# An attention and recurrence trunk on one core: PSUM banks of the dense units in turns, products from GpSimd to VectorE, key copies one by one

## Chip, cores and metric

One core of one Trainium2 chip. The metric is the time of one execution on the device in microseconds. The kernel before takes 905.94 us, the median of 3 runs (905.71 to 905.98).

## What is computed

Two layers over x (1024 tokens x 1024 features, float32), each with a normalisation before and after and a residual:

```
for layer in range(2):
    h = rmsnorm(x, pre_norm_w[layer])
    y = attention_mixer(h) if layer == 0 else hgrn2_mixer(h)
    x = x + rmsnorm(y, post_norm_w[layer])

attention_mixer:
    q, k, v, z = split(h @ w_in + b_in)            # 1024, 128, 128, 1024 wide
    q, k = partial_rope(q), partial_rope(k)        # 16 query heads, 2 key heads of 64
    o = softmax over the last 128 keys, with a learned sink per head, times v
    return (o * silu(z)) @ w_out + b_out
```

The second layer is a gated linear recurrence with projections of the same kind; the change does not touch it.

## The kernel before, in words

**Dense work.** Every projection is made of units: 8 "products" (steps over the 1024 features) of 3 matmuls each, which accumulate a 128x512 result in one PSUM bank. Each float32 operand is split into a high and a low part (hi, lo), and the three matmuls are hi·hi, hi·lo and lo·hi. A unit is one block of 128 output features and one half (512) of the tokens (`proj_feat`), or 128 tokens and 512 output features (`proj_nat`). `product` (L218 of the profile; in stretches in which TensorE's order is pinned, all its matmuls appear as L88) counts products in `W["pos"]`. Weights come by DMA into `wraw`, and are split into `whi` (L177 on GpSimd, L179 on ScalarE) and `wlo` (L180 on VectorE).

**PSUM.** The 8 banks are four tags of two banks: "mm" for dense units, "s" for scores, "t" for transposes, "o" for outputs. `mm()` hands a dense unit its bank. A bank comes free when its last reader is done; with two banks of a tag a third user waits for the first one's reader.

**Attention.** The stage of layer 0 weaves attention blocks into the dense units. Before its loop of units, the first half's units run (v, q and k of tokens 0 to 511). Then `fill` lists the rest, in order: the second half's key unit and value unit, four query units of head group 0 for the second half, eight query units of group 1, sixteen gate units (z), then four output units. Beside it stands a plan, a list of (product count, function): after each product the entries that have come due are issued. Block number i (of 32: 2 head groups x 8 query blocks x 2 parities) is due at 29 + 7.1 i products with `scores` (8 matmuls into "s", copy and mask L695/L699, minimum L703, exponentials L705, L707, scaling L710 or L712), 13 products later with `turned` (4 transposes into "t", split by L721 on ScalarE and L722 on VectorE, masks L728 to L736 on GpSimd), and 22 products later with `heads_out` (3 or 4 matmuls into "o", read by L754 and L755). In head group 1 the second parity is followed by L757 on GpSimd, the product of gate and output.

**Query units** (`q_unit`) read the bank with L431 (qh, ScalarE) and L433 (ql, VectorE). For the rotary block (ct 0) the chain is: L422 on ScalarE reads the bank, L424 makes the sine product in two pieces on VectorE, L425 the cosine product in place on GpSimd, L426 adds on VectorE, L427 and L429 split. The parts are stored to DRAM (L436) and loaded again block by block (`queries`, L669). **The key unit** (`k_unit`) reads its bank with L557, rotates on VectorE (L558, L562, L563) and copies each key head's 64 rows to both partition halves: KH on ScalarE (L568), KL on VectorE (L569). In the second half these copies wait in the plan, two pairs per entry, at 30 and 36 products after the unit, and each is queued on ScalarE behind the latest exponential. **The value unit** reads its bank with L587 (vf). **Gate units** (`z_unit`) make L641 (ScalarE), L642 (GpSimd), L646 (VectorE) and, for the group whose output is there already, L648 on GpSimd: output times gate. `new_og` closes the pool with the key work's tiles and opens the tile of group 1's outputs in its place.

**What sets the order.** TensorE's order in this stage is the order of the program. The other engines' queues are ordered by the tile scheduler from priorities and its own simulated times, with the bank's readers at high priority, and run in that fixed order on the chip.

Of the kernel before, what the change touches and what calls it, by code (L numbers as in the profile page):

```python
# [12 lines left out]
F32 = mybir.dt.float32  # L13
# [4 lines left out]
AF = mybir.ActivationFunctionType  # L18
ALU = mybir.AluOpType
# [71 lines left out]
def emit(tc, I, out):  # L91
    nc = tc.nc
    v = InOrder(tc, nc.vector)
# [7 lines left out]
    with top:  # L101
# [13 lines left out]
        pos = const.tile([P, 64], I32, name="pos")  # L115
# [14 lines left out]
        whi = [wp.tile([P, 512], F32R, name=f"whi{i}") for i in range(NW)]  # L130
        wlo = [wp.tile([P, 512], F32R, name=f"wlo{i}") for i in range(NW)]
        wraw = [wp.tile([P, 512], F32, name=f"wraw{i}") for i in range(NR)]
        NS = I["w"].shape[0]
        W_K = 10
        W = {"pos": 0, "plan": [], "split": 0, "fetch": 0, "left": {}, "place": {}, "dmas": {}, "split_ins": {}, "free": list(zip(whi, wlo))}


        FIRST = (0, 2, 1, 3)
# [71 lines left out]
            v.scalar_tensor_tensor(lo, ps, scale, hi.bitcast(F32), op0=ALU.mult, op1=ALU.subtract)  # L210

        def mm(shape=(P, 512), tag="mm"):
            return pp.tile(list(shape), F32, tag=tag, name="psmm")

        def product(ps, k, stat, mov):
# [8 lines left out]
        def later(d, f, block=99):  # L224

            W["plan"].append((W["pos"] + d, f, block))
            W["plan"].sort(key=lambda e: e[0])
# [145 lines left out]
        def layer0():  # L373
# [3 lines left out]
            cosT = ka.tile([P, T], F32, tag="big0", name="cosT")  # L377
# [4 lines left out]
            KH = base.tile([P, 2, T], F32R, name="KH")  # L382
            KL = base.tile([P, 2, T], F32R, name="KL")
# [19 lines left out]
            def q_unit(g, ct, half, ps=None, at=None, sc=None):  # L403
                if ps is None:
                    ps = proj_feat(q_first(g, ct), half)
                with hp():
                    b = bias(2 + 4 * g + ct)
                    cs = slice(half * 512, (half + 1) * 512)
                    if sc is None:
                        sc = scaled(ps, half)  # L410
                    ps = sc
                    if at is None:
                        qh = ka.tile([P, 512], F32R, tag="qh", bufs=2, name="qh")
                        ql = None
                    else:
                        qh, ql = [o0v[:, at + i, :].bitcast(F32R) for i in range(2)]
                    hs = slice(8 * g, 8 * g + 8)
                    own = lambda x: ql if ql is not None else x.bitcast(F32R)
                    if ct == 0:
                        qf = qp.tile([P, 512], F32, tag="th", bufs=3, name="qf") if half else ps  # L420
                        tB = qp.tile([P, 512], F32, tag="th", bufs=3, name="qtB")
                        nc.scalar.activation(qf, ps, AF.Identity, bias=b)  # L422
                        for o, i in ((0, 64), (64, 0)):
                            v.tensor_tensor(tB[o:o + 64], qf[i:i + 64], sinT[o:o + 64, cs], op=ALU.mult)  # L424
                        nc.gpsimd.tensor_tensor(qf, qf, cosT[:, cs], op=ALU.mult)  # L425
                        v.tensor_tensor(qf, qf, tB, op=ALU.add)  # L426
                        nc.scalar.activation(qh, qf, AF.Copy)  # L427
                        ql = own(qf)
                        v.tensor_tensor(ql, qf, qh.bitcast(F32), op=ALU.subtract)  # L429
                    else:  # L430
                        nc.scalar.activation(qh, ps, AF.Identity, bias=b)  # L431
                        ql = own(qp.tile([P, 512], F32, tag="th", bufs=3, name="ql") if half else ps)
                        v.scalar_tensor_tensor(ql, ps, b, qh.bitcast(F32), op0=ALU.add, op1=ALU.subtract)  # L433
                    for l, q in enumerate((qh, ql)):
                        for k, (r, n) in enumerate((((0, 8), (32, 8)), ((8, 16),), ((24, 8), (40, 8)), ((48, 16),))[ct]):
                            nc.sync.dma_start(qdh[hs, 64 * l + r:64 * l + r + n, cs], q[64 * k:64 * k + 8 * n].bitcast(F32))  # L436
# [3 lines left out]
            with pool("start", "right") as sp:  # L440
# [109 lines left out]
                def k_unit(half):  # L550
                    cs = slice(half * 512, (half + 1) * 512)
                    ps = proj_feat(W_K, half)
                    with hp():
                        ps = scaled(ps, half)
                        kr = qp.tile([P, 512], F32, tag="th", bufs=3, name="kr") if half else ps

                        nc.scalar.activation(kr, ps, AF.Identity, bias=hbias[:, 0:1], scale=-0.125)  # L557
                    v.tensor_tensor(kf, kr, cosK[:, cs], op=ALU.mult)  # L558
                    for o in range(4):
                        s1, s2 = slice(32 * o, 32 * o + 8), slice(32 * (o ^ 1), 32 * (o ^ 1) + 8)  # L560
                        s3 = slice(64 * (o % 2), 64 * (o % 2) + 8)
                        v.tensor_tensor(tK[s1], kr[s2], sinT[s3, cs], op=ALU.mult)  # L562
                    v.tensor_tensor(kf, kf, tK, op=ALU.add)  # L563

                    def halves(kv):
                        kr = kf[64 * kv:64 * kv + 64]
                        for o in (0, 64):
                            nc.scalar.activation(KH[o:o + 64, kv, cs], kr, AF.Copy)  # L568
                            v.tensor_tensor(KL[o:o + 64, kv, cs], kr, KH[o:o + 64, kv, cs].bitcast(F32), op=ALU.subtract)  # L569

                    for kv in range(2):
                        if half:
                            def behind(kv):

                                with tc.issue_after(W["exp"].ins):
                                    halves(kv)
                            later(30 + 6 * kv, lambda kv=kv: behind(kv))
                        else:
                            halves(kv)

                def v_unit(half, ps=None, sc=None):
                    if ps is None:
# [52 lines left out]
            with pool("att", "right") as ap:  # L635
                def z_unit(p, half):
                    ps = proj_feat(20 + 2 * (p ^ 4), half)
                    with hp():
                        ps = scaled(ps, half)
                        th = ka.tile([P, 512], F32, tag="qh", bufs=2, name="th")  # L640
                        nc.scalar.activation(th, ps, AF.Tanh, bias=hbias[:, 10 + p:11 + p], scale=0.5)  # L641
                        nc.gpsimd.tensor_scalar(th, th, 0.5, 0.5, op0=ALU.mult, op1=ALU.add)  # L642
                        o = og[p // 4][:, p % 4, half * 512:(half + 1) * 512]

                        early = p >= 4
                        v.scalar_tensor_tensor(o if early else th, ps, bias(10 + p), th, op0=ALU.add, op1=ALU.mult)  # L646
                        if not early:
                            nc.gpsimd.tensor_tensor(o, o, th, op=ALU.mult)  # L648

                og = [o0]  # L650
                qdr = qd.rearrange("(h r) t -> r h t", r=P)
# [88 lines left out]
                def heads_out(g, b, par):  # L740
                    o = par * 64
                    if par == 0:
                        obs[g, b] = qp.tile([P, 4, P], F32, tag="ob", bufs=1, name="ob")
                    ob, ogb = obs[g, b], og[g][:, :, b * P:(b + 1) * P]
                    pT, mY = pTs.pop((g, b, par))
                    pTh, pTl = pT[:, 0], pT[:, 1]
                    po = pp.tile([P, 4, P], F32, tag="o", name="pso")
                    x = VX[:, b, g].rearrange("p a d -> p (a d)")
                    pe.matmul(po, x, pTh, start=True, stop=False)
                    pe.matmul(po, x, pTl, start=False, stop=False)  # L750
                    if b > 0:
                        pe.matmul(po[:, :, :64], tw[b][0], mY[:, :, :64], start=False, stop=False)
                    pe.matmul(po[:, :, 64:], tw[b][1], mY[:, :, 64:], start=False, stop=True)
                    nc.scalar.activation(ob[o:o + 64], po[64:128], AF.Copy)  # L754
                    v.tensor_tensor((ob if g else ogb)[o:o + 64], po[0:64], ob[o:o + 64], op=ALU.add)  # L755
                    if par and g:
                        nc.gpsimd.tensor_tensor(ogb, ogb, ob, op=ALU.mult)  # L757

                qs = lambda g, h: [lambda ct=ct: q_unit(g, ct, h) for ct in (1, 0, 2, 3)]
                zs = lambda *u: [lambda p=p, h=h: z_unit(p, h) for p, h in u]  # L760
                def new_og():
# [2 lines left out]

                q1 = [lambda ct=ct, h=h: q_unit(1, ct, h)
                      for ct, h in ((0, 0), (1, 0), (0, 1), (1, 1), (2, 0), (2, 1), (3, 0), (3, 1))]
                fill = [lambda: k_unit(1), lambda: v_unit(1)] + qs(0, 1) + [new_og] + q1
                fill += zs((4, 0), (4, 1), (5, 0), (5, 1), (6, 0), (7, 0), (6, 1), (7, 1))
                fill += zs(*[(p, h) for h in range(2) for p in range(4)])
                order = [(g, b) for g in range(2) for b in range(8)]  # L770
# [486 lines left out]
```

## Time and profile before

| | |
|---|---|
| median of 3 runs | 905.94 us |
| the profiled execution | 905.04 us |
| its span, first to last instruction | 903.2 us |
| granted TensorE clock, mean | 0.997 |

In the rows below each instruction has its start in us, its length, its engine (PE TensorE, DVE VectorE, ACT ScalarE, POOL GpSimd), its source line, and "out<-in" with the program's tile names. Brackets hold the idle time of the engine just before, and what ended it. Rows of waits have the total, the number and the longest. Matmuls are pipelined: the length of a row is longer than the distance from one matmul's start to the next one's.

### The profile page before, as it was taken

Reading aid. Unit: us, or ns where it says so; the run is one execution under the profiler, and the core shown is the slowest. Engines: PE = TensorE matmul, PEld = TensorE weight load, DVE = VectorE, ACT = ScalarE, POOL = GpSimd, SP = SyncE. Lnnn points to the kernel's source line nnn. Section 1 sums busy time; section 2 is a strip of 40 time slices with the busy share of each in tenths; the row PEclk is TensorE's granted clock in tenths of the full one; section 3 lists DMA queues with packets and bytes.
Section 4 is the critical chain, followed back from the end, with each engine's and each line's share of the span. In section 5 each row is a group of like instructions: output and inputs, shape, how many; then the busy total and the mean of one; then the engine's idle time right before and its main releaser. Section 6 shows DMA issues by size and latency. Waiting matters only on the chain.

```text
span 903.2 us, 14308 instructions
## 1 busy us (share of the span) xinstructions
PE 877.7 (97%) x5286; PEld 731.5 (81%) x5286; DVE 548.6 (61%) x880; ACT 401.1 (44%) x1048; POOL 346.8 (38%) x512
## 2 busy tenths in 40 slices
PE   6998999999999999999999999999999999999996
PEld 5877888888887878788888888888888788888885
DVE  7988787676788336752278873336877824252343
ACT  5734777767787332542322432333334224251211
POOL 4542565666898303420153522115434433220011
PEclk9999999999999999999999999999999999999998
DMA  9765465323132134531311010211111003031053
GB/s 341 269 187 153 142 187 152 86 55 96 54 91 83 47 94 142 184 107 49 91 49 34 15 48 1 78 53 35 35 37 48 2 1 94 1 122 65 24 187 120
DMA packets 55639, 82.61 MB, mean 91 GB/s; under 512 B 5128, under 2 KB 25224, under 8 KB 55560
## 3 DMA queue, kind: packets, MB, share of 16 engines
q1 hardware_dynamic: 55280, 81.54, 28.8%
q8 instruction: 43, 0.70, 0.3%
q14 instruction: 36, 0.29, 0.1%
q10 hardware_dynamic: 280, 0.07, 0.0%
HBM read 62.88 MB, written 16.88 MB: 88 GB/s over the span
## 4 chain that ended last, share of the span: by engine, by line
PE 77%; DVE 9%; issue 5%; POOL 4%; ACT 3%; DMA 1%; DVEq 0%; SPq 0%; POOLq 0%; ACTq 0%
PE psmm L218 48%; PE psmm L88 17%; PE pss L88 2%; PE pso L88 2%; POOL rstd L256 2%; PE psk L1041 1%; PE pso L1054 1%; PE pso L1056 1%; PE pst L88 1%; POOL ms L254 1%; ACT sm L705 1%; DVE wlo L180 1%; DMA wraw<-in_w 1%; PE pst L1035 1%; DVE actl L790 1%
## 5 line engine op out<-in xcount | busy, mean ns | idle before, releaser
L218 PE MATMUL psmm<-whi,acth 128*128 128x512 f32 (+1 forms) x488 | 190.6, 392 | 1.1 <-DVE y L820 1.1
L218 PE MATMUL psmm<-whi,actl 128*128 128x512 f32 (+1 forms) x488 | 188.8, 388 | 0.0
L218 PE MATMUL psmm<-wlo,acth 128*128 128x512 f32 (+1 forms) x488 | 188.8, 387 | 0.0
L180 DVE TENSOR_TENSOR wlo<-wraw,whi 128x512 fp32r<-128x512 f32 x120 | 90.3, 764 | 94.8 <-ACT whi L179 91.3
L88 PE MATMUL psmm<-acth,whi 128*128 128x512 f32 x272 | 110.8, 407 | 5.9 <-DVE ql L433 2.8
L179 ACT ACTIVATE whi<-wraw 128x512 fp32r<-128x512 f32 x112 | 70.1, 630 | 88.0 <-PE psmm L218 66.9
L218 PEld LDWEIGHTS psmm<-whi,acth 128*128 128x128 f32 x488 | 91.7, 188 | 20.7 <-DVE y L820 1.8
L88 PE MATMUL psmm<-actl,whi 128*128 128x512 f32 x272 | 107.5, 395 | 0.2 <-DVE actl L88 0.2
L88 PE MATMUL psmm<-acth,wlo 128*128 128x512 f32 x272 | 107.6, 395 | 0.0
L218 PEld LDWEIGHTS psmm<-whi,actl 128*128 128x128 f32 x488 | 91.7, 188 | 18.3
L218 PEld LDWEIGHTS psmm<-wlo,acth 128*128 128x128 f32 x488 | 91.8, 188 | 17.8
L218 PE MATMUL psmm<-acth,whi 128*128 128x512 f32 x256 | 101.1, 395 | 0.2 <-DVE qf L894 0.2
L218 PE MATMUL psmm<-acth,wlo 128*128 128x512 f32 x256 | 100.4, 392 | 0.0
L218 PE MATMUL psmm<-actl,whi 128*128 128x512 f32 x256 | 100.3, 392 | 0.0
L705 ACT ACTIVATE sm<-sm,st 128x129 f32<-128x129 f32 x128 | 50.0, 392 | 36.1 <-DVE st L703 35.6
L88 PEld LDWEIGHTS psmm<-acth,whi 128*128 128x128 f32 x272 | 51.8, 191 | 15.5 <-DVE ql L433 3.6
L902 POOL TENSOR_SCALAR gate<-gate,lbt 128x512 f32<-128x512 f32 x16 | 17.7, 1108 | 119.4 <-ACT gate L900 108.9
L88 PEld LDWEIGHTS psmm<-acth,wlo 128*128 128x128 f32 x272 | 51.6, 190 | 11.5 <-DVE wlo L88 0.2
L88 PEld LDWEIGHTS psmm<-actl,whi 128*128 128x128 f32 x272 | 51.7, 190 | 8.7 <-DVE actl L88 1.0
L218 PEld LDWEIGHTS psmm<-acth,whi 128*128 128x128 f32 x256 | 48.1, 188 | 10.8 <-DVE qf L894 0.9
L218 PEld LDWEIGHTS psmm<-acth,wlo 128*128 128x128 f32 x256 | 48.1, 188 | 10.0
L218 PEld LDWEIGHTS psmm<-actl,whi 128*128 128x128 f32 x256 | 48.1, 188 | 9.4
(268 smaller groups left out, 1630.7 us busy)
## 6 DMA issues: line engine op xcount, KB each, us to landing
wraw<-in_w SPq DMA_DIRECT2D x132, 256.0 KB
QS<-qd SPq DMA_DIRECT2D x16, 512.0 KB
xr<-in_x SPq DMA_DIRECT2D x8, 512.0 KB
x1d<-xn SPq DMA_DIRECT2D x8, 512.0 KB
xr<-x1d SPq DMA_DIRECT2D x8, 512.0 KB
out_dram<-xn SPq DMA_DIRECT2D x16, 256.0 KB
o<-in_xt SPq DMA_DIRECT2D x8, 256.0 KB
xt<-in_x SPq DMA_DIRECT2D x4, 512.0 KB
```

The lines of the kernel that those rows point to most:

```text
L88: return (lambda *a, **k: self.tc.keep_in_program_order(f(*a, **k))) if self.on else f
L179: nc.scalar.activation(hi, raw, AF.Copy)
L180: W["split_ins"][i] = v.tensor_tensor(lo, raw, hi.bitcast(F32), op=ALU.subtract)
L218: W["mm"] = pe.matmul(ps, a, b, start=(k == 0 and i == 0), stop=(k == NK - 1 and i == 2))
L254: keep(g.tensor_scalar(m, ms, eps, 1.0, op0=ALU.add, op1=ALU.mult))
L256: W["rstd"] = keep(g.tensor_tensor(r, m, nhalf[:, :width], op=ALU.pow))
L705: W["exp"] = nc.scalar.activation(sm[:, h, :], sm[:, h, :], AF.Exp, bias=nm[:, h:h + 1], scale=-1.0, accum_out=dn[:, h:h + 1])
L790: v.tensor_tensor(lo, o, hi.bitcast(F32), op=ALU.subtract)
L902: nc.gpsimd.tensor_scalar(dst, dst, ol, lb, op0=ALU.mult, op1=ALU.add)
L1035: nc.tensor.transpose(pt[:, i, :], Y[:, c * P:(c + 1) * P], ident)
L1041: nc.tensor.matmul(pk[:, i, :], yn[:, c, :], vt[:, c, hc], start=True, stop=True)
L1054: nc.tensor.matmul(po[:, i, :], sc[:, c, :], vt[:, c, hc], start=True, stop=(c == 0))
```

## The change

Four edits, all in the attention stage. While the plan has entries, `mm()` ignores the tag it is given and takes banks from the tags in turns: t, mm, o, mm. The cosine product of the rotary query units (4 of them, one before the loop) and the products L648 (8) and L757 (8) go from GpSimd to VectorE. The second half's key copies are four plan entries of one pair each, at 31, 35, 39 and 43 products after the unit, rather than two entries of two pairs at 30 and 36. `new_og` comes behind the first three of group 1's query units.

```
         def mm(shape=(P, 512), tag="mm"):
+            if W["plan"]:
+                W["bank"] += 1
+                tag = ("mm", "t", "mm", "o")[W["bank"] % 4]
             return pp.tile(list(shape), F32, tag=tag, name="psmm")
...
-                        nc.gpsimd.tensor_tensor(qf, qf, cosT[:, cs], op=ALU.mult)
+                        v.tensor_tensor(qf, qf, cosT[:, cs], op=ALU.mult)
...
-                    def halves(kv):
+                    def halves(kv, o):
                         kr = kf[64 * kv:64 * kv + 64]
-                        for o in (0, 64):
-                            nc.scalar.activation(KH[o:o + 64, kv, cs], kr, AF.Copy)
-                            v.tensor_tensor(KL[o:o + 64, kv, cs], kr, KH[...], op=ALU.subtract)
+                        nc.scalar.activation(KH[o:o + 64, kv, cs], kr, AF.Copy)
+                        v.tensor_tensor(KL[o:o + 64, kv, cs], kr, KH[...], op=ALU.subtract)
...
-                    for kv in range(2):
+                    for i in range(4):
                         if half:
...
                                 with tc.issue_after(W["exp"].ins):
-                                    halves(kv)
-                            later(30 + 6 * kv, lambda kv=kv: behind(kv))
+                                    halves(i // 2, i % 2 * 64)
+                            later(31 + 4 * i, lambda i=i: behind(i))
...
                         if not early:
-                            nc.gpsimd.tensor_tensor(o, o, th, op=ALU.mult)
+                            v.tensor_tensor(o, o, th, op=ALU.mult)
...
                     if par and g:
-                        nc.gpsimd.tensor_tensor(ogb, ogb, ob, op=ALU.mult)
+                        v.tensor_tensor(ogb, ogb, ob, op=ALU.mult)
...
-                fill = [lambda: k_unit(1), lambda: v_unit(1)] + qs(0, 1) + [new_og] + q1
+                fill = [lambda: k_unit(1), lambda: v_unit(1)] + qs(0, 1) + q1[:3] + [new_og] + q1[3:]
```

More of the change, by code (lines that the diff above doesn't have):

```diff
@@ L134, in emit @@
         W_K = 10
-        W = {"pos": 0, "plan": [], "split": 0, "fetch": 0, "left": {}, "place": {}, "dmas": {}, "split_ins": {}, "free": list(zip(whi, wlo))}
+        W = {"pos": 0, "bank": 0, "plan": [], "split": 0, "fetch": 0, "left": {}, "place": {}, "dmas": {}, "split_ins": {}, "free": list(zip(whi, wlo))}
         FIRST = (0, 2, 1, 3)
@@ L563, in k_unit, with behind @@
                     v.tensor_tensor(kf, kf, tK, op=ALU.add)
-                    def halves(kv):
+                    def halves(kv, o):
                         kr = kf[64 * kv:64 * kv + 64]
-                        for o in (0, 64):
-                            nc.scalar.activation(KH[o:o + 64, kv, cs], kr, AF.Copy)
-                            v.tensor_tensor(KL[o:o + 64, kv, cs], kr, KH[o:o + 64, kv, cs].bitcast(F32), op=ALU.subtract)
-                    for kv in range(2):
+                        nc.scalar.activation(KH[o:o + 64, kv, cs], kr, AF.Copy)
+                        v.tensor_tensor(KL[o:o + 64, kv, cs], kr, KH[o:o + 64, kv, cs].bitcast(F32), op=ALU.subtract)
+                    for i in range(4):
                         if half:
-                            def behind(kv):
+                            def behind(i):
                                 with tc.issue_after(W["exp"].ins):
-                                    halves(kv)
-                            later(30 + 6 * kv, lambda kv=kv: behind(kv))
+                                    halves(i // 2, i % 2 * 64)
+                            later(31 + 4 * i, lambda i=i: behind(i))
                         else:
-                            halves(kv)
+                            halves(i // 2, i % 2 * 64)
                 def v_unit(half, ps=None, sc=None):
```

## Prediction

> **What bounds the kernel now.** I read the page first, then the busy time by stages, then TensorE's waits inside the one stage that the change touches, then the engines' instructions around each wait.
>
> ```profile
> span 903.2 us, 14308 instructions
> PE 877.7 (97%) x5286; PEld 731.5 (81%) x5286; DVE 548.6 (61%) x880; ACT 401.1 (44%) x1048; POOL 346.8 (38%) x512
> ```
>
> TensorE (PE) is busy 97% of the span; no other engine is over 61%. So time is to be had only where PE waits, and every other engine matters as far as it makes PE wait. The attention stage is the part of the span up to 313 us. Busy time in three stretches of it (columns: the stretch and its length, then PE, PEld, DVE, ACT, POOL, the granted clock, the DMA share, GB/s):
>
> ```profile
> 55.00:106.00 51.00, 46.26 (x233) 37.62 (x232) 44.10 (x78) 28.48 (x83) 19.02 (x30) 1.00 0.50 147
> 106.00:235.00 129.00, 129.00 (x689) 109.94 (x688) 92.02 (x168) 95.76 (x296) 80.46 (x145) 1.00 0.41 116
> 235.00:286.00 51.00, 49.11 (x261) 40.93 (x259) 45.27 (x71) 40.58 (x116) 44.70 (x63) 1.00 0.26 72
> ```
>
> The middle 129 us have no idle PE at all. The two ends have: there VectorE (DVE) is at 44.10 and 45.27 of 51, about 88%, and at the late end GpSimd (POOL) is as full, 44.70. The granted clock is 1.00 throughout. TensorE's waits between 55 and 313 us (total, times, longest):
>
> ```profile
> PE psmm L88 <- DVE ql L433: 2.8, 2, 2.2
> PE pso L88 <- POOL pT L736: 1.5, 2, 0.9
> PE psmm L88 <- ACT vf L587: 1.4, 1, 1.4
> PE pss L88 <- DVE sm L699: 0.9, 2, 0.6
> ```
>
> These four are 6.6 us, the whole stock that the change can take from. The first and third are a dense unit (24 matmuls into psmm) that waits for a PSUM bank: the two "mm" banks are both held, one by the unit just finished, the other by the unit before, whose reader (vf, ql) is late. Measured from matmul to matmul:
>
> ```profile
> 60.22 0.39 PE L88 MATMUL psmm<-actl,whi 128*128 128x512 f32 x1
> 60.45 0.39 PE L88 MATMUL psmm<-acth,wlo 128*128 128x512 f32 x1
> 62.24 0.50 PE L88 MATMUL psmm<-acth,whi 128*128 128x512 f32 x1 [1.41 <-ACT vf L587]
> 69.08 0.39 PE L88 MATMUL psmm<-acth,wlo 128*128 128x512 f32 x1
> 70.04 0.50 PE L88 MATMUL psmm<-acth,whi 128*128 128x512 f32 x1 [0.57 <-DVE ql L433]
> 83.52 0.39 PE L88 MATMUL psmm<-acth,wlo 128*128 128x512 f32 x1
> 86.13 0.50 PE L88 MATMUL psmm<-acth,whi 128*128 128x512 f32 x1 [2.22 <-DVE ql L433]
> ```
>
> Pace is 0.23 us a matmul (60.22 to 60.45). The three starts come 1.79, 0.96 and 2.61 us after their predecessors: 1.56 + 0.73 + 2.38 = 4.7 us lost at bank waits, all before 87 us. With the other two waits the stock is 4.7 + 1.5 + 0.9 = 7.1 us.
>
> **Edit 1, banks in turns.** From the second half's key unit on, units take t, mm, o, mm and so on. An "mm" unit now waits for the unit four before it, a "t" or "o" unit for whatever transposes or outputs hold. At the three waits above the units are v_unit's second successor (now mm, its older bank that of k_unit(0), long read), the next (t) and the second after (o). All three conditions are met well before 60, 69 and 83 us, so all 4.7 us leave these places. What is late next? In the order of PE: the transposes of the first softmax block, then those of the second, which need a t bank while a dense unit holds one.
>
> ```profile
> 77.91 0.60 PE L88 MATMUL pst<-cst,sm 128*128 128x128 f32 x4
> 87.63 0.60 PE L88 MATMUL pst<-cst,sm 128*128 128x128 f32 x4
> 85.33 0.74 DVE L433 SCALAR_TENSOR_TENSOR ql<-psmm,cst,qh 128x512 fp32r<-128x512 f32 x1
> 86.75 0.69 DVE L722 TENSOR_TENSOR pT<-pst,pT 128x512 fp32r<-128x512 f32 x1 [0.67 <-ACT pT L721]
> 115.90 0.60 PE L88 MATMUL pst<-cst,sm 128*128 128x128 f32 x4
> 119.79 0.68 DVE L722 TENSOR_TENSOR pT<-pst,pT 128x512 fp32r<-128x512 f32 x1
> ```
>
> The first transposes hold their bank from 77.91 to 87.44; the dense unit in the other t bank is read until 86.07 (85.33 + 0.74). PE would reach the second transposes at 87.63 - 4.7 = 82.9. If nothing else moved it would stand there until 86.07, and 3.1 of the 4.7 us would be given back. So edit 1 alone is worth 1.6 us; the rest hangs on edits 2 and 3. In the middle stretch transposes hold a bank 4.6 us (115.90 to 120.47) at a spacing of about 7 us, so one t bank serves them there.
>
> **Edits 2 and 3, where that bank is late.** Rows of POOL, DVE and ACT before 86 us:
>
> ```profile
> 77.67 1.28 POOL L425 TENSOR_TENSOR qf<-qf,cosT 128x512 f32<-128x512 f32 x1 [4.13 <-DVE qtB L424]
> 76.12 1.40 DVE L424 TENSOR_TENSOR qtB<-qf,sinT 64x512 f32<-64x512 f32 x2
> 80.83 0.68 DVE L426 TENSOR_TENSOR qf<-qf,qtB 128x512 f32<-128x512 f32 x1
> 82.56 1.27 ACT L568 ACTIVATE KH<-kft 64x512 fp32r<-64x512 f32 x2
> 83.86 0.63 ACT L427 ACTIVATE qh<-qf 128x512 fp32r<-128x512 f32 x1
> 84.40 0.67 ACT L431 ACTIVATE qh<-psmm,cst 128x512 fp32r<-128x512 f32 x1
> ```
>
> The reader L431/L433 stands in ACT's queue behind the pair of key copies (1.27) and behind L427, which needs L426, which needs the cosine product from POOL. On DVE that product is one more 128x512 operation between L424 and L426, 0.60 us from start to start: L426 could start at 77.52 + 0.60 = 78.1 in place of 80.83, 2.7 earlier. Keys one by one put one copy (0.63) in place of two ahead of L427: 0.6 earlier. Together 3.3, against the 3.1 that are needed. A further help comes earlier still:
>
> ```profile
> 45.78 1.71 DVE L424 TENSOR_TENSOR qtB<-sc,sinT 64x512 f32<-64x512 f32 x2
> 50.52 0.76 POOL L354 TENSOR_SCALAR cosK<-cosT,cst 128x512 f32<-128x512 f32 x1 [4.28 <-DMA cosT<-csd]
> 51.24 1.29 POOL L425 TENSOR_TENSOR sc<-sc,cosT 128x512 f32<-128x512 f32 x1
> 52.56 0.69 DVE L426 TENSOR_TENSOR sc<-sc,qtB 128x512 f32<-128x512 f32 x1 [3.49 <-POOL sc L425]
> ```
>
> The first half's cosine stands in POOL's queue behind cosK, which waits for a DMA, and DVE idles 3.49 us for it. On DVE it costs 0.60 inside that idle time, so up to 2.9 us of DVE's backlog before 74 us go, and with them lateness of what follows on DVE. The three cosines before 106 us (51.24, 77.67 and, below, 100.74) cost 3 x 0.60 = 1.8 us of DVE, less than the idle time that they end. The order on each queue is made anew by the scheduler, which no row shows, so I leave 1.0 of the 4.7 as waits in new places (bounds 0 and 3.1). **Edits 1 to 3: 3.7 us.** The key copies now come at products 39, 43, 47 and 51 instead of 38 and 44; nothing reads the second half's keys before product 86, some 30 us later. Each copy queues behind an exponential on ACT, as before. Moving new_og behind three units issues nothing, its tile is first written eight units later: zero. No DMA is moved past another; query stores follow qh, which comes earlier.
>
> **Edit 4, cosine and gate products off POOL in the loop.** PE's wait for POOL's masks (L736, 1.5 us in two pieces) comes where a cosine or a gate product stands ahead of the masks in POOL's queue:
>
> ```profile
> 100.74 1.28 POOL L425 TENSOR_TENSOR sc<-sc,cosT 128x512 f32<-128x512 f32 x1
> 274.48 1.67 POOL L648 TENSOR_TENSOR o<-o,th 128x512 f32<-128x512 f32 x1 [0.71 <-DVE th L646]
> 280.09 1.24 POOL L736 TENSOR_SCALAR_AFFINE_SELECT pT<-pT 128x512 fp32r<-128x512 f32 x1
> L757 POOL TENSOR_TENSOR og<-og,ob 128x512 f32<-128x512 f32 x8 | 11.7, 1463 | 2.7 <-DVE ob L755 2.7
> L648 POOL TENSOR_TENSOR o<-o,th 128x512 f32<-128x512 f32 x8 | 11.2, 1396 | 2.2 <-DVE th L646 1.3 <-DVE st L707 0.9
> 242.28 1.75 POOL L757 TENSOR_TENSOR og<-og,ob 128x512 f32<-128x512 f32 x1
> 242.99 1.58 DVE L712 TENSOR_TENSOR sm<-sm,st 128x512 f32<-128x512 f32 x1
> 119.18 0.69 DVE L712 TENSOR_TENSOR sm<-sm,st 128x512 f32<-128x512 f32 x1
> ```
>
> Sixteen products, 22.9 us, leave POOL. From 235 to 286 us six L648 and three L757 run: POOL falls from 44.70 by 9 x 1.4 = 13 to 32, so I count its 1.5 us as gone. DVE gains 9 x 0.60 = 5.4 us. But L712 took 1.58 us while L757 ran on POOL and 0.69 us alone: a POOL product costs DVE up to 0.9 us. If half of the nine do, DVE gets 4.0 back, and its load goes from 45.3 to about 46.7 of 51. I charge 0.3 us of new waits for that and leave the 0.9 us at L699 standing. Bounds: all of L699's 0.9 gained too, or 5.4 lost. In the middle stretch DVE has 129 - 92 = 37 us idle to hide the rest. **Edit 4: 1.2 us.** The Trainium skill (SBUF — State Buffer, Who interferes with whom) says a VectorE instruction with two SBUF inputs contends with a GpSimd one that reads SBUF, and the loser blocks. The L712 rows agree. The rule also speaks against the edit: the moved products have two SBUF inputs themselves and meet POOL's masks, and the sum by it is the second rival's.
>
> Sum: 3.7 + 1.2 = 4.9 us. The profiled execution took 905.04 (its span 903.2 and 1.8 outside); the median of the runs is 905.94, 0.9 over it. After 313 us PE is the bound again (its work there is untouched), so the gain is carried to the end: 905.9 - 4.9 = **901.0 us**.
>
> **Rivals.** *Gain given back.* The readers keep their place in the queues, PE stops at the second transposes (3.1 back), and at the late end DVE's waits take POOL's place: 1.6 us are left, 904.3. For: the 9.5 us hold of the first transposes. Against: the 3.3 us worked out above. Chance 0.15.
>
> *VectorE becomes the bound, slower.* At the late end DVE's 5.73 us idle are dependences that stay, and 5.4 us of products come on top without the stretch going, since POOL's masks now collide with the moved products; POOL's 1.5 are gained. In front 1.6 is left and two cosines in the loop cost 1.2. That is 905.9 + 5.4 - 1.5 - 1.6 + 1.2 = 909.4. It decides if a moved product takes over about 1.2 us on DVE, double its 0.60. For: 88% load at both ends. Against: the stretch that the rows show is 0.9 at most, and beside a product on POOL. Chance 0.09. The Trainium skill (Perfetto Trace Analysis, Optimizing Scalar/DVE Operations) warns in this sense that shifting work between GPSIMD and DVE might not help, as they share a read port.
>
> *More than the stock.* All 7.1 us go and the later stages are ordered better: 898 or less, chance 0.06. That the rotation isn't in force I exclude: the list that switches it on is filled before the first unit that counts.
>
> **How the numbers follow.** The forecast (3 to 7.1 us gained) has 0.70. The range 898 to 905 leaves out the third rival, all of the slower one and the end of the first: about 0.19. A measurement tells about 0.2%, 1.8 us, from no change. Faster by more: 0.70 + 0.06 + a quarter of the first rival = 0.80; within: 0.12; slower: 0.08.
>
> **What would show it.** Right: no wait of psmm on vf or ql between 55 and 106 us; PE's waits there under 1.5 us; the 3.49 us idle at L426 gone; L427 within 2 us of L424; POOL under 34 of 51 us at the late end and no pso wait on L736; moved products at 0.7 to 1.0 us on DVE. Wrong: pst waiting for L722 or L433 (edit 1 given back), pss or pst waiting for L699 or L712 by over 2 us (DVE the bound), or a stage after 313 us that is longer.

## The result, and the profile after

The kernel after takes 899.93 us, the median of 4 runs, against 905.9 before: a ratio of 0.9937 (95% interval 0.9925 to 0.995), 6.0 us less. A second set of 5 runs beside other kernels gave 900.42 and 0.9935 (0.9921 to 0.9949). Forecast were 901.0 us, with a range of 898 to 905.

The profiled execution took 900.95 us. Its span and busy time from the page:

```profile
span 899.1 us, 14318 instructions
PE 878.8 (98%) x5286; PEld 732.2 (81%) x5286; DVE 556.3 (62%) x900; ACT 401.5 (45%) x1048; POOL 326.1 (36%) x492
```

TensorE has the same work in 4.1 us less span. Twenty operations have gone from POOL to DVE: 7.7 us more there, 20.7 us less on POOL. The stretches that answer to the three shown of before (same columns):

```profile
55.00:104.00 49.00, 47.77 (x238) 38.64 (x237) 43.59 (x76) 29.28 (x84) 17.84 (x30) 1.00 0.53 157
104.00:232.00 128.00, 128.00 (x681) 108.74 (x680) 95.75 (x174) 94.99 (x295) 73.81 (x138) 1.00 0.40 116
232.00:282.00 50.00, 49.67 (x262) 41.42 (x261) 46.91 (x81) 42.01 (x119) 35.89 (x55) 1.00 0.27 77
```

PE's idle time in front fell from 4.7 to 1.2 us, at the late end from 1.9 to 0.3. TensorE's waits in the whole stage after (total, times, longest):

```profile
PE pst L88 <- ACT sm L713: 1.0, 1, 1.0
PE pss L88 <- DVE sm L702: 0.2, 1, 0.2
```

Of 6.6 us of waits 1.2 are left, and no dense unit waits for a bank. (Lines behind an edit are 3 or 4 higher than in the kernel before: L713 is the scaling, L710 before; L429 the cosine product, L425 before.) The larger of the two waits left is at the second softmax block's transposes, as forecast, but not for a bank. The matmul ahead of it, the wait, and ScalarE's queue up to the scaling:

```profile
82.85 0.39 PE L88 MATMUL psmm<-acth,wlo 128*128 128x512 f32 x1
84.21 1.20 PE L88 MATMUL pst<-cst,sm 128*128 128x128 f32 x4 [0.98 <-ACT sm L713]
```

```profile
81.46 1.27 ACT L571 ACTIVATE KH<-kft 64x512 fp32r<-64x512 f32 x2
82.75 0.60 ACT L724 ACTIVATE pT<-pst 128x512 fp32r<-128x512 f32 x1
83.25 0.62 ACT L179 ACTIVATE whi<-wraw 128x512 fp32r<-128x512 f32 x1
83.77 1.26 ACT L713 ACTIVATE sm<-sm,st 128x128 f32<-128x128 f32 x4
```

Four scalings run one head after the other and the four transposes follow at their pace, 1.20 us in place of 0.60. In front of them in ScalarE's queue stand two key copies, a split of transposes and a weight split: the scheduler put two of the single entries in a row again. The slower pace costs another 0.60 us that no row of waits holds.

What the first half's cosine product did on VectorE and, behind it, on ScalarE and TensorE. Before, from the key rotation to the bank's reader:

```profile
53.17 0.70 DVE L558 TENSOR_TENSOR kft<-sc,cosK 128x512 f32<-128x512 f32 x1
58.89 2.59 ACT L568 ACTIVATE KH<-kft 64x512 fp32r<-64x512 f32 x4 [0.99 <-DVE kft L563]
61.50 0.69 ACT L587 ACTIVATE vf<-psmm,cst 128x512 f32<-128x512 f32 x1
```

After:

```profile
49.37 0.69 DVE L429 TENSOR_TENSOR sc<-sc,cosT 128x512 f32<-128x512 f32 x1
49.97 0.16 DVE L300 TENSOR_TENSOR lm<-cst 128x8 f32<-128x8 f32 x1
50.04 0.68 DVE L562 TENSOR_TENSOR kft<-sc,cosK 128x512 f32<-128x512 f32 x1
...
54.08 0.69 DVE L430 TENSOR_TENSOR sc<-sc,qtB 128x512 f32<-128x512 f32 x1
```

```profile
56.87 2.58 ACT L571 ACTIVATE KH<-kft 64x512 fp32r<-64x512 f32 x4
59.48 0.69 ACT L590 ACTIVATE vf<-psmm,cst 128x512 f32<-128x512 f32 x1
```

```profile
61.13 0.39 PE L88 MATMUL psmm<-acth,whi 128*128 128x512 f32 x1
```

The 3.49 us idle before the addition are gone. In the old order DVE's next work, the key rotation, stood behind that addition; now it starts at 50.04 instead of 53.17, and the addition comes after it. The first KH copies start 2.0 us sooner, and vf is read at 60.17 (62.19 before), where the unit that used to wait for its bank starts at 61.13.

The traces show 4.1 us, the medians 6.0. The profiled execution of before (905.04) was below all its timed runs (905.71 to 905.98), that of after was the slowest of its own (900.95; another profiled execution of the same kernel took 900.42 with a span of 898.7). Part of the difference is the start: dense unit five begins at 33.93 us in the first trace of after and at 33.45 in the second. Against that second trace the span is 4.5 us shorter than before.

### The profile page after: what moved, and what is told of

It is laid out like the page before. It is cut to its first block, busy times and chain, and to the rows that moved or that the text cites. A ratio compares the mean times of both kernels' runs of the same rounds, so it can differ in the third digit from the quotient of the medians.

```text
span 899.1 us, 14318 instructions
## 1 busy us (share of the span) xinstructions
PE 878.8 (98%) x5286; PEld 732.2 (81%) x5286; DVE 556.3 (62%) x900; ACT 401.5 (45%) x1048; POOL 326.1 (36%) x492
## 4 chain that ended last, share of the span: by engine, by line
PE 78%; DVE 8%; issue 4%; DMA 4%; POOL 3%; ACT 1%; SPq 0%; DVEq 0%; POOLq 0%; ACTq 0%
PE psmm L222 48%; PE psmm L88 16%; PE pss L88 3%; PE pso L88 2%; DMA wraw<-in_w 2%; POOL rstd L260 2%; PE psk L1044 1%; PE pst L88 1%; PE pso L1057 1%; PE pso L1059 1%; POOL ms L258 1%; DMA xt<-in_xt 1%; PE pst L1038 1%; PE pst L1071 1%; DVE actl L88 1%
## 5 line engine op out<-in xcount | busy, mean ns | idle before, releaser
L180 DVE TENSOR_TENSOR wlo<-wraw,whi 128x512 fp32r<-128x512 f32 x120 | 87.6, 740 | 94.1 <-ACT whi L179 88.6
```

The lines of the kernel that those rows point to most:

```text
L180: W["split_ins"][i] = v.tensor_tensor(lo, raw, hi.bitcast(F32), op=ALU.subtract)
```

## Experiments

After the result there were two theories. The **bank theory** is the prediction's: the rotation removes the bank waits, and the other edits keep them from coming back. The **reader theory** says that the banks were never short: their readers were late, and once the cosine product has brought the readers forward, two banks do. Each kernel's time is a median; the ratio is to the kernel before, run beside it (905.65 us for e1 to e4, 906.14 for e5 to e7 and the kernel after again, 906.13 for e8 to e11). A table at the end of the section compares stretches of the traces.

**e1, the rotation alone**, in the kernel before:

```
 def mm(shape=(P, 512), tag="mm"):
+    if W["plan"]:
+        W["bank"] += 1
+        tag = ("mm", "t", "mm", "o")[W["bank"] % 4]
```

> The kernel before with the rotation of banks alone. Bank theory (the prediction's edit 1): the three bank waits of 4.7 us leave their places, 3.1 come back at the second transposes, so 1.6 us are gained: 904.3. Reader theory (the late readers were the cause, and rotation only hides them): PE meets the same late readers through other waits, gain under 1 us, 905 to 906. If the rotation alone carried the change it would be near 900.

905.37 us, 0.9996 (0.9987 to 1.0005): no change. TensorE's waits between 55 and 309 us:

```profile
PE pss L88 <- DVE sm L703: 3.2, 5, 1.1
PE pso L88 <- POOL pT L740: 1.4, 2, 0.9
PE pst L88 <- DVE ql L437: 1.0, 1, 1.0
PE pst L88 <- POOL vmid L599: 0.8, 1, 0.8
PE psl L88 <- POOL vmid L596: 0.2, 1, 0.2
```

The psmm waits (4.2 us by the wait rows of before) are gone, and 4.3 have taken their place: 2.3 more at the scores, whose bank DVE reads late, 1.0 at the transposes for ql (the place that the prediction named), 1.0 at the value unit's transposes. PE comes sooner to an engine that is not sooner. The reader theory's number was met.

**e2, everything but the rotation**: the three lines above taken out of the kernel after.

> The kernel after without the rotation: dense units keep the two mm banks. Bank theory: the bank waits of 4.7 us come back in large part, 903 to 904.5. Reader theory: in the trace of the kernel after, vf is read by 60.17 and its two-bank user starts at 61.13, ql by 68.05 against 68.46, the next ql by 81.23 against 81.71, so two banks would do: 900 to 900.7, and no psmm wait over 0.5 us between 55 and 106 us.

900.23 us, 0.9935 (0.9922 to 0.9949), the same ratio as with it.

```profile
PE pss L88 <- DMA QS<-qd: 1.2, 1, 1.2
PE pss L88 <- DVE sm L698: 0.5, 2, 0.3
PE pst L88 <- ACT sm L709: 0.3, 1, 0.3
```

With two banks no dense unit waits for one, and the reader theory's number was met. The bank theory falls with these two runs. A new name stands on top: the first scores wait for the queries' load. In the trace the front is 0.8 us longer than in the kernel after, which the medians don't show; whether the rotation is worth some tenths beside the other edits stays open.

**e3, the four cosine products back on POOL**, in the kernel after: `nc.gpsimd.tensor_tensor(qf, qf, cosT[:, cs], ...)`.

> The kernel after with the four cosine products back on GpSimd. Both theories have the cosine chain as what makes the readers late. Bank theory: with rotation kept, only the 2.7 us by which L426 moved are lost at the second transposes, less what the key copies give: 901.5 to 902.5. Reader theory: DVE idles 3.5 us again before 53 us and everything behind it is late: 902.5 to 904.

903.48 us, 0.9971 (0.996 to 0.9981). Against the kernel after (0.9935 to 0.9937) they carry some 3.2 us, and the reader theory's number was met. PE's waits are again those of e1: 2.2 at the scores, 1.0 for ql, 0.6 for vmid.

**e10, the first half's cosine back on POOL**: `(v if half else nc.gpsimd).tensor_tensor(qf, qf, cosT[:, cs], ...)`. The expectation below counts one product. The edit moves two: `half` is 0 for the unit ahead of the loop and for group 1's rotary unit of tokens 0 to 511, in the loop. POOL has 494 instructions against 492 in the kernel after.

> The kernel after with only the first half's cosine product (one of four, ahead of the loop) back on GpSimd, where it stands behind the cosK product that waits for a DMA. Reader theory: this one product frees 2.9 us of VectorE's backlog, so most of the 3.2 us that all four are worth go with it: 902.3 to 903.2. Rival, the three in the loop matter as much each: 900.7.

904.36 us, 0.9983 (0.9974 to 0.9992): slower than the reader theory's number. The addition that waits for the first product, and the second product:

```profile
52.57 0.69 DVE L430 TENSOR_TENSOR sc<-sc,qtB 128x512 f32<-128x512 f32 x1 [3.64 <-POOL sc L429]
101.21 1.29 POOL L429 TENSOR_TENSOR sc<-sc,cosT 128x512 f32<-128x512 f32 x1
```

```profile
PE pss L88 <- DVE sm L702: 2.0, 3, 0.9
PE pso L88 <- POOL pT L739: 1.4, 1, 1.4
PE pst L88 <- POOL vmid L598: 0.5, 1, 0.5
PE pst L88 <- ACT sm L713: 0.5, 1, 0.5
PE psl L88 <- POOL vmid L595: 0.2, 1, 0.2
```

Two products out of twenty moved operations hold about 4 us by the medians. The trace tells them apart. From one and the same matmul near 43 us to one near 98 us TensorE takes 55.5 us here and 52.4 to 52.5 in the kernel after, and the second product starts only behind that: some 3.1 us belong to the first one. Its 3.64 us idle time is back, and so are the waits behind it. The second product stands ahead of the masks that PE waits for at 105 us (1.4), and the stretch there is 0.6 us longer. With all four back (3.2 us in e3, with intervals that overlap) no more is lost, so no run shows a gain of the two in the second half.

**e11, the four cosine products alone**, in the kernel before, on VectorE.

> The kernel before with the four cosine products on VectorE and nothing else. Reader theory: the readers come sooner and two banks do, so the cosines alone carry 3 us: 902.5 to 903.2, and the psmm waits on vf and ql are gone or under 0.5 us. Bank theory: without rotation the bank waits stay for the most part, 904.5 to 905.5.

902.34 us, 0.9957 (0.9943 to 0.9971): 3.8 us from one word in one line, a little more than the reader theory's number.

```profile
PE pso L88 <- POOL pT L736: 1.2, 2, 0.9
PE pss L88 <- DVE sm L699: 1.0, 2, 0.7
PE pss L88 <- DMA QS<-qd: 0.4, 1, 0.4
```

The bank waits on vf and ql are gone without a bank more. In the trace the front is 3.3 us shorter than in the kernel before, against 3.0 and 3.1 in the two traces of the kernel after: the cosines alone carry all that the change gains there. What is left are mainly waits at the late end, where edit 4 aims.

**e4, the sixteen gate products back on POOL**, in the kernel after (both lines `v` to `nc.gpsimd`).

> The kernel after with the sixteen gate products back on GpSimd. Prediction: 1.2 us of the gain (POOL's masks 1.1 at 280 us, less 0.3 of VectorE) go: about 900.8 to 901.1, with PE waiting for L736's masks again near 276 us. Rival, VectorE's load costs as much as POOL's relief gives: 899.9, no difference.

901.33 us, 0.9947 (0.9934 to 0.9961).

```profile
PE pss L88 <- DVE sm L702: 1.0, 2, 0.7
PE pst L88 <- ACT sm L713: 1.0, 1, 1.0
PE pso L88 <- POOL pT L739: 0.9, 1, 0.9
```

The interval overlaps that of the kernel after; the trace decides. POOL's masks are waited for again (0.9), and the scores wait 0.8 more. The same three dense units of the late end run from 257.29 to 283.17 us here, from 260.12 to 285.98 in the kernel before, and from 257.67 to 282.20 in the kernel after: 25.9, 25.9 and 24.5. All ten traces with these products on VectorE have 24.5 there, and all four with them on POOL 25.8 to 25.9. Up to a matmul 33 us further on, 0.3 us more are gained. So the edit is worth 1.3 us at the late end and 1.7 in all, against 1.2 forecast; the median lies a little above the expected 901.1.

**e5, key copies in pairs again**: entries at 30 and 36 products that issue two copies each.

> The kernel after with the second half's key copies in two entries of two pairs at 30 and 36 products again. Prediction: a pair costs 0.63 us more of ScalarE ahead of the reader of the bank that the second transposes wait for, so up to 0.6 us slower, 900.5. Rival: in the trace of the kernel after two copies still run in a row (1.27 us at 81.46), so single entries changed nothing there and the time stays at 899.9.

901.55 us, 0.9947 (0.9934 to 0.9961), 1.1 over the kernel after beside it, with overlapping intervals, and above both numbers. Its waits are different ones (0.6 at the second transposes, 0.6 at outputs) but hardly more in sum. In the trace it keeps up to 95 us and then takes 28.5 us to the outputs at 123.69, where the kernel after takes 27.3. So single copies seem to be worth 1.1 us in this kernel, far behind the place that the prediction priced; it is one trace, and why stays open.

**e6, key copies 14 products later**: `later(45 + 4 * i, ...)`.

> The kernel after with the key copies 14 products later (45, 49, 53, 57 products after the unit; their first reader is at product 86). In the kernel after PE stands 1.1 us at the second transposes for the scaling on ScalarE, which is queued behind two key copies (1.27 us). Queue theory: without them the scaling is 1.27 us sooner and the wait goes: 898.8 to 899.2. Rival, the exponentials or VectorE's reciprocal are what is late: 899.9.

903.02 us, 0.9966 (0.9954 to 0.9978): slower, and neither number was met. The wait that the theory spoke of did go: no PE wait is left before 109 us. But the last copy fell into the next rotary unit's chain on ScalarE, and PE waited there. The wait, and PE's granted clock around it (the first number behind the five engines', 1.00 being full speed):

```profile
121.39 1.09 PE L88 MATMUL pst<-cst,sm 128*128 128x128 f32 x4 [2.45 <-ACT sm L708]
```

```profile
114.00:118.00 4.00, 4.00 (x20) 3.32 (x20) 3.97 (x8) 3.21 (x11) 2.08 (x4) 1.00 0.63 196
118.00:122.00 4.00, 1.55 (x8) 1.08 (x7) 3.42 (x8) 2.60 (x12) 1.79 (x3) 0.87 0.52 148
122.00:126.00 4.00, 4.00 (x19) 3.52 (x18) 1.59 (x3) 2.63 (x7) 1.94 (x6) 0.70 0.58 168
126.00:130.00 4.00, 4.00 (x21) 3.27 (x21) 3.24 (x6) 3.15 (x11) 1.19 (x2) 1.00 0.04 17
```

The wait cost more than its 2.45 us: the granted clock was 0.70 in the stretch behind it.

**e7, the scaling of block 0's second parity on VectorE**: `if par and (g, b) != (0, 0):` ahead of the four scalings.

> The kernel after, with the scaling of block 0's second parity on VectorE (one operation of about 0.7 us) in place of four on ScalarE. Queue theory: the scaled rows are there at about 82.5 us, before PE comes (83.1), and its 1.1 us wait and the slow pace of the four transposes (0.7) go: 898.2 to 899. Rival, VectorE has no room and its later work is late by as much: 899.9 or more.

899.44 us, 0.9927 (0.9913 to 0.994), between the two numbers. The transposes' wait is gone, and most of it is met again one step on, at the next scores:

```profile
PE pss L88 <- DVE sm L702: 1.5, 2, 1.3
```

**The kernel after again**, beside e5 to e7:

> The kernel after, unchanged, beside the others: 899.9. Its profiled execution took 900.95 where its other runs took 899.8 to 899.98; if that is the start-up pace of the first matmuls (0.43 us each up to 13.9 us), another profile ends that pace at another time and the span differs by as much.

900.42 us; the second profile's start-up pace ended sooner (11.5 us against 13.5), as expected.

**e8, key copies 6 products later**: `later(37 + 4 * i, ...)`.

> The kernel after with the key copies 6 products later (37, 41, 45, 49 after the unit). With them 14 later the front wait of 1.8 us was gone, but the last copy stood at 108.7 us in the chain of the next rotary unit and PE waited 2.8 us at 118.6. Queue theory: copies that fall between the two rotary units (89 to 98 us) cost PE nothing: 898 to 898.8. Rival, any place of the copies costs a wait somewhere, since ScalarE's and VectorE's order is made anew: 899.9 or more.

899.98 us, 0.9932 (0.9919 to 0.9946), not to be told from the kernel after; the rival's number was met. The front wait is gone, and in its place come slow transposes at 96.7 us and, for once, a dense unit that waits for a transposes' bank:

```profile
98.11 0.50 PE L88 MATMUL psmm<-acth,whi 128*128 128x512 f32 x1 [0.33 <-DVE pT L725]
```

That is the price of the rotation which the prediction feared, at 0.33 us.

**e9, key copies at 44 to 53 products**: `later(44 + 3 * i, ...)`.

> The kernel after with the key copies at 44, 47, 50, 53 products after the unit: later than in the run with 37, and the last one sooner than in the run with 45. Queue theory: the last copy falls before 102 us, ahead of the next rotary unit's chain, so neither wait appears: 898 to 898.8. If the last copies still fall behind the exponentials of product 65, near 108 us, PE waits again at 118 us: 901.5 to 903.

899.29 us, 0.9927 (0.9912 to 0.9941), the best median of all, but not under 898.8.

```profile
PE pss L88 <- DMA QS<-qd: 0.6, 1, 0.6
PE pss L88 <- DVE sm L702: 0.2, 1, 0.2
```

Only 0.8 us of waits are left in the stage. Its lead over the kernel after is of the size that the medians vary by (0.9927 against 0.9935, intervals overlapping); the traces have it 1.6 us shorter than the second one of after (897.1 against 898.7). e7 and e9 were not tried together.

**The same stretches in all traces.** TensorE's 5286 matmuls stand in the same order in every run, so the time between the same two can be compared, whatever the pace at the start. The 151st, 401st and 542nd matmul start at 42.77, 98.56 and 125.59 us in the kernel before, and the 1259th and 1383rd are the two of e4's measure:

| kernel | 151st to 401st | 401st to 542nd | 1259th to 1383rd |
|---|---|---|---|
| before | 55.80 | 27.03 | 25.87 |
| after | 52.47 | 27.33 | 24.53 |
| after again | 52.35 | 27.33 | 24.53 |
| e1, rotation alone | 56.38 | 27.06 | 25.92 |
| e2, no rotation | 53.29 | 27.25 | 24.50 |
| e3, four cosines back | 55.89 | 27.12 | 24.50 |
| e10, two cosines back | 55.54 | 27.92 | 24.50 |
| e11, cosines alone | 51.78 | 27.77 | 25.83 |
| e4, gate products back | 52.09 | 27.33 | 25.88 |
| e5, keys in pairs | 52.34 | 28.48 | 24.51 |

The first two columns together are the front: 82.8 us before, 79.8 and 79.7 after, 79.6 in e11.

## Why the prediction came out as it did

**What bounds the kernel: right.** The stock was PE's waits in this stage, 7.1 us, and the gain came out of this stage: what lies behind it is as long as it was (313 to 903 us before, 309 to 899 after).

**Edit 1, wrong.** The step that failed is "edit 1 alone is worth 1.6 us; the rest hangs on edits 2 and 3". It followed the bank waits to the next place in PE's order where a bank is short, and stopped at the one that it found, 3.1 us. e1 shows that all of it comes back, 1.0 at the place that it found and the rest at other waits on DVE and POOL, and e2 that the change does as well without the rotation. Here the wait for a bank was a wait for the bank's reader. The prediction had the reader's lateness in its rows and still gave the credit to the bank. Its rival "gain given back" comes nearest to e1, though it left 1.6 us and e1 left none; it does not describe the change.

**Edit 2, right in its mechanism and mis-sized.** The first cosine product was priced as up to 2.9 us of backlog, "a further help", beside the loop's cosine at 2.7 us. e10 puts the first one at some 3.1 us in front, out of the 3.0 and 3.1 that the whole change gains there, and e3 shows nothing for the second half's. By the rows, what stood behind it moved with it: the key rotation on DVE, then the KH copies and vf on ScalarE, each 2 to 3 us sooner. Not all signs held. In the loop the split of the rotary block came 2.8 us behind the sine products, not within 2, since a weight split and masked copies of scores were put between.

**Edit 3, priced at the wrong place.** 0.6 us were given for one copy in place of two ahead of the bank's reader. On the chip two copies stand in a row still (81.46), now ahead of the scaling. What e5 loses it loses behind 95 us, and e11 has the whole gain in front with the copies in pairs.

**The sum in front** was 4.7 less 1.0 left over, 3.7 us; the traces have 3.0 and 3.1. Left over are 1.0 us of wait and 0.6 of slow pace, at the transposes forecast, for another reason: the scaling, not the bank. That the 1.0 was met is luck.

**Edit 4, right way and near in size, by other parts.** The sum was 1.5 us at POOL's masks less 0.3 of new waits. e4 finds 1.3 us at the late end: 0.9 at the masks and 0.8 at the scores, which the sum had left standing, less some slower transposes (1.21 us in place of 0.60 for a block's four at 267.38). DVE's price, group rows after:

```profile
L760 DVE TENSOR_TENSOR og<-og,ob 128x512 f32<-128x512 f32 x8 | 6.9, 860 | 0.1
L651 DVE TENSOR_TENSOR o<-o,th 128x512 f32<-128x512 f32 x8 | 5.4, 680 | 0.0
```

These are means of 0.68 and 0.86 us; three of the eight L760 took 1.10 to 1.16, over the sign's 1.0 and near the 1.2 at which the slower rival decides. DVE's load at the late end is 46.91 of 50 us. POOL's is 35.89, where 32 were expected and under 34 was the sign. The twenty products took 28.1 us on POOL, but POOL's busy time fell by 20.7: its other instructions took some 7 us longer in all. They cost DVE 15.1 us, but its busy time rose by 7.7, as its other instructions took some 7 us less. The prediction's sum counted part of the second and nothing of the first.

**So the total** was near (4.9 against 4.1 and 4.5 in the traces and 6.0 in the medians) because the waits' stock was read rightly. The larger part of it was put down to the wrong edit, and that the terms add up to nearly the right sum is partly luck.

## What to carry to other kernels

Before giving a waiting engine more buffers, ask why the reader is late, and test the buffers alone: here the turns over more banks bought nothing, and one operation taken out of a queue that waited for a DMA bought some two thirds of the gain. Look for an operation that idles a busy engine early in a stage: what stands behind it in that engine's fixed order, and behind that on other engines, moves with it, and here some 3.1 of the 3.5 us of idle time came out as gain. Read from the trace that an edit moved what you meant it to move: e10 moved two products where one was meant. Moving work in a scheduled queue by a few steps can cost as much as it gains (e6 against e9), so try several places.

## What the runs showed of the hardware

A wait of 2.45 us on PE (2.8 from matmul to matmul) was followed by a lower granted clock in e6: 0.70 from 122 to 126 us, with the first dense matmuls there 0.43 us apart instead of 0.23. The wait of 2.22 us in the kernel before (2.61 from matmul to matmul) was not: there dense matmuls came 0.23 apart at once. The Trainium skill (TensorE: Matmul & The Clock Gate, HAM oscillation — how this bites in real kernels) speaks of idle gaps over some 3.4 us; here a shorter one was enough once, and one a little shorter still was not. The same halved pace, 0.43 us, holds at the start of the traces and ends 11 to 14 us in; two traces of one kernel begin the same unit 0.5 us apart for it.
